# The attention's loads of K, Q, V and the bias table move from SP's DMA queue to GpSimd's

## The chip, the core and the metric

The kernel runs on one core of a Trainium2 chip. PE (TensorE) multiplies matrices and loads its weights beside that (PEld); DVE (VectorE), ACT (ScalarE) and POOL (GpSimd) work on tiles in on-chip memory; SP (SyncE) issues DMAs. Each engine works through its own instructions in order, and waits on semaphores for the others. The metric is the device time of one execution in microseconds (us), less is better.

## What is computed

Two groups of tokens (512 and 2048, treated as five chunks of 512: chunk 0 is the prompt, chunks 1 to 4 are the sample) go through one encoder layer of width 1024. One projection of the normed input gives all branch inputs and gates. Branch A is neighbourhood attention of eight heads on a grid 64 tokens wide (each query sees a window of 8 x 16), branch B the real part of a 2-D DFT, branch C a gated depthwise convolution of width 31. The three are merged under sigmoid gates.

```python
def encoder_layer(x, ...):
    h = rms_norm(x, pre_g)
    z = h @ w_in
    (q, k, v, gate_a, u_b, gate_b, c_val, c_glu, gate_c,
     merge_a, merge_b, merge_c) = jnp.split(z, split_pts, axis=-1)
    y_a = neighbourhood_attention(heads(q), heads(k), heads(v), rpb) * jax.nn.silu(gate_a)
    y_b = fourier_mix(u_b) * jax.nn.silu(gate_b)
    y_c = conformer_conv(c_val, c_glu, dw_w, dw_b, cn_g, cn_b) * jax.nn.silu(gate_c)
    merged = (jax.nn.sigmoid(merge_a) * (y_a @ w_a)
              + jax.nn.sigmoid(merge_b) * (y_b @ w_b)
              + jax.nn.sigmoid(merge_c) * (y_c @ w_c))
    return x + rms_norm(merged @ w_o, post_g)
```

All is float32; the big products are made of three matmuls of split operands (a high part and a remainder).

## The kernel before

**Projections.** `narrow` (L171 to L182) and `wide` multiply the normed chunks `hT` with weights; an output block of `narrow`, 128 x 512, takes 24 matmuls, eight each of L178, L179 and L180. Weights come by `emit_unit` (L138): SP loads 512 KB into a ring `wraw` of three buffers (L142), and ACT and DVE split them (L134, L135). Projections go in three stages: chunks 1 and 2, then 3 and 4, then 0. Each stage makes K, Q, V, the DFT's input and the gates and writes them to DRAM.

**Attention.** `attention(c)` reads them back, for each of eight heads and in each for four column blocks: `load` brings K (`ksp`, L524), Q (`qsp`, two DMAs, L528) and the bias table (`tab`, L530) of the next head, `load_v` brings V (`vsp`) by 8 DMAs of 64 KB (L540) in chunks 2 and 3, by 16 DMAs (L545) in the others. POOL adds table and mask to a `bias` (L560 in chunks 2 and 3, L563 in the others; two buffers, one block ahead). PE multiplies Q and K (L592, tile `s`), DVE adds the bias and takes the maximum `m` (L596), ACT exponentiates and scales (L600, L602), PE transposes (L623), DVE splits (L626), PE multiplies with V (L634), and SP stores the result (L644).

**DFT.** `fft` loads its input (`fu`, L664), and then works in units: a table `w` of 1 MB (L730, one buffer), a matmul L750 (`hp`, in the same two PSUM buffers as the attention's `s`), a second L765, additions on DVE, and a store of the result `yb` (L789). It runs for two halves of the channels, once for chunks 1 to 4 (five units a half), and then for chunk 0 (two units a half).

**Norms.** `rstd_rows` writes the norms of a chunk to DRAM (`rs`, L211), `make_h` reads them back as a row in all partitions (`rrow`, L217), and DVE multiplies the input with it (L221).

**What sets the order.** Projections call `pump()` every few matmuls, and `pump` lets side tasks (attention, convolution, DFT, norms) emit their next piece in proportion. A task has a first and a last step: the attention of chunk 1 is spread over 240 steps, that of chunks 2, 3 and 4 together over 280, that of chunk 0 over 56, and the DFT of chunk 0 comes at the end. What is emitted in this order is then scheduled: the framework simulates the program and sets from that the order of each engine's instructions, so a change of an instruction's engine can move others. Tiles wait for the readers of their buffer's last content.

**The merge.** After chunk 0's projections come the merge and the last projection (`prepare` with L801 to L807, `merge`, `finish`), whose matmuls of `ysp` and `wb` (L178 to L180 in the shape 128x256) begin the stage. Their weights `wb` (L1051) share the ring `wraw` with the projections' weights.

Of the kernel before, what the change touches and what calls it, by code (L numbers as in the profile page):

```python
# [15 lines left out]
F32 = mybir.dt.float32  # L16
# [87 lines left out]
class Build:  # L104
# [399 lines left out]
    def attention(self, c):  # L504

        nc, pool = self.nc, self.ap
        nq, trow, krow = PATS[c]
        n, rows = nq * P, 4 * nq
        kds, vds = self.kds[c > 0], self.vds[c > 0].rearrange("(r w) d -> r w d", w=64)
        grouped = nq == 4  # L510
        mask = pool.tile([P, 3, 512], BF16, tag="mask", name="mask", bufs=1)
        nc.sync.dma_start(mask, self.a["mask"][MASKPAT[c]])
        tq, vq, ahead = [], [], []
        tabs, qk, vs, obs = {}, {}, {}, {}

        def load(hh):


            if hh > 7:
                return  # L520
            j, h = hh // 2, hh % 2
            ksp = pool.tile([P, 16 * 64], F32R, tag="ksp", name="ksp", bufs=2)
            src = kds[j, h].rearrange("i p t -> (i p) t")[:, krow * 64: krow * 64 + rows * 64]
            nc.sync.dma_start(ksp[:, :rows * 64].bitcast(F32), src)  # L524
            qsp = pool.tile([P, 2, C], F32R, tag="qsp", name="qsp", bufs=2)
            src = self.qd[c][j][:, h * 64: h * 64 + 64].rearrange("i p t -> p i t")
            for half in (slice(0, 64), slice(64, P)):
                nc.sync.dma_start(qsp[half].bitcast(F32), src)  # L528
            tb = pool.tile([P, 6, 16, 8], F32, tag="tab", name="tab", bufs=2)
            nc.sync.dma_start(tb, self.a["tab"][hh])  # L530
            qk[hh] = ksp, qsp.rearrange("p i (b q) -> p i b q", b=4)
            tabs[hh] = tb

        def load_v(hh):

            cols = slice(hh * P, hh * P + P)
            vsp = pool.tile([P, 12, P], F32R, tag="vsp", name="vsp", bufs=2)
            if grouped:
                for g in range(8):
                    nc.sync.dma_start(vsp[:, g].bitcast(F32), vds[krow: krow + rows, 8 * g: 8 * g + 8, cols])  # L540
            else:
                for cb in range(4):
                    for r in range(4):
                        src = vds.rearrange("(q r) w d -> r w q d", r=4)
                        nc.sync.dma_start(  # L545
                            vsp[32 * r: 32 * r + 32, nq * cb: nq * cb + nq].bitcast(F32),
                            src[r, KSTART[cb]: KSTART[cb] + 32, krow // 4: krow // 4 + nq, cols])
            vs[hh] = vsp

        def biases():  # L550
            for hh in range(8):
                for cb in range(4):
                    bias = pool.tile([P, 512], F32, tag="bias", name="bias", bufs=2)
                    g0 = RCOL[cb] // 8
                    t = tabs[hh][:, g0: g0 + 4, trow: trow + rows]
                    m, b = mask[:, COLPAT[cb], :n], bias[:, :n]
                    if grouped:
                        m, b = (x.rearrange("p (g r w) -> p g r w", g=4, w=8) for x in (m, b))
                        m, b, t = (x.rearrange("p g r w -> p g (r w)") for x in (m, b, t))
                        nc.gpsimd.tensor_tensor(b, t, m, op=ALU.add)  # L560
                    else:
                        m, b = (x.rearrange("p (r g w) -> p g r w", g=4, w=8) for x in (m, b))
                        nc.gpsimd.tensor_tensor(b, t, m, op=ALU.add)  # L563
                    yield bias

        gen = biases()

        def make_bias():
            return next(gen, None)

        load(0)
        ahead.append(make_bias())
        for _ in range(3):
            yield
        for hh in range(8):
            ksp, qsp = qk.pop(hh)
            for cb in range(4):
                if cb == 1:
                    load(hh + 1)
                if cb == 2:  # L580
                    load_v(hh)
                if cb % 2 == 0:
                    pv = self.ps.tile([P, 2, 2, P], F32, tag="o", name="pv", bufs=1)
                if cb == 0:
                    obs[hh] = pool.tile([P, C], F32, tag="o", name="ob", bufs=2)
                bias = ahead.pop(0)
                ahead.append(make_bias())
                s = self.ps.tile([P, 512], F32, tag="s", name="s", bufs=2)
                kk = ksp.rearrange("p (r c) -> p r c", c=64)[:, :rows, KSTART[cb]: KSTART[cb] + 32]
                if grouped:  # L590
                    kk = kk.rearrange("p r (g w) -> p g r w", w=8)
                nc.tensor.matmul(s[:, :n], lhsT=qsp[:, 0, cb], rhs=kk, start=True, stop=False)  # L592
                nc.tensor.matmul(s[:, :n], lhsT=qsp[:, 1, cb], rhs=kk, start=False, stop=True)
                p = pool.tile([P, 512], F32, tag="p", name="p", bufs=3)
                m = pool.tile([P, 4], F32, tag="m", name="m", bufs=4)
                nc.vector.tensor_tensor_reduce(  # L596
                    out=p[:, :n], in0=s[:, :n], in1=bias[:, :n], scale=1.0, scalar=-3e38,
                    op0=ALU.add, op1=ALU.max, accum_out=m[:, 0:1])
                nc.vector.tensor_scalar_mul(m[:, 1:2], m[:, 0:1], -1.0)  # L599
                nc.scalar.activation(p[:, :n], p[:, :n], AF.Exp, bias=m[:, 1:2], accum_out=m[:, 2:3])  # L600
                nc.vector.reciprocal(m[:, 3:4], m[:, 2:3])
                nc.scalar.mul(p[:, :n], p[:, :n], m[:, 3:4])  # L602
                tq.append(partial(self.transpose_p, nq, p, c, hh, cb, vs, pv, obs))
                yield
                if len(tq) > 3:
                    vq.append(tq.pop(0)())
                yield
                if len(vq) > 2:
                    vq.pop(0)()
                yield  # L610
        while tq or vq:
            if vq:
                vq.pop(0)()
                yield
            if tq:
                vq.append(tq.pop(0)())
                yield
# [526 lines left out]
```

## Time and profile before

| | |
|---|---|
| median of 3 runs (lowest to highest) | 2137.19 us (2135.92 to 2137.59) |
| the profiled execution's own time | 2136.65 us |
| its span in the trace | 2134.8 us |
| mean granted clock of PE | 0.987 |
| busy: PE, PEld | 2069.1 us (97%), 1775.8 us (83%) |
| busy: DVE, ACT, POOL | 1300.3 us (61%), 795.8 us (37%), 292.8 us (14%) |
| moved by DMA | 389.33 MB, mean 182 GB/s |

The span reaches from the first to the last instruction in the trace; the rest of the execution's own time lies around it. SP is not among the busy engines: an issue of a DMA isn't counted as busy, but it holds the queue for the time that its row gives. The granted clock is a share of full speed: 1 is 2.4 GHz, 0.5 is 1.2 GHz, and what lies between is a mixture within the stretch.

### The profile page before, as it was taken

The numbers are of one execution on the slowest core, as the hardware profiler recorded it, in microseconds if no ns is written. First come the engines' busy times: TensorE is split into PE (matmuls) and PEld (weight loads), VectorE is DVE, ScalarE is ACT, GpSimd is POOL, SyncE is SP. The second block draws the span as 40 slices with busy tenths as digits, with TensorE's granted clock in tenths as the row PEclk, the third lists the DMA queues.
The fourth block names the chain that finished last, engine by engine and source line by source line (L and its number), as shares of the span: only waits on it lengthen the run. The fifth ranks groups of instructions, "written<-read, shape, count | busy, mean of one in ns | idle before, by whom it ended". The sixth has DMA issues, their size and how long they took to land. (4 is left out here: it accounts for less than half of the span.)

```text
span 2134.8 us, 31256 instructions
## 1 busy us (share of the span) xinstructions
PE 2069.1 (97%) x11184; PEld 1775.8 (83%) x11184; DVE 1300.3 (61%) x2850; ACT 795.8 (37%) x1625; POOL 292.8 (14%) x286
## 2 busy tenths in 40 slices
PE   8999999999979999999999969999889999999998
PEld 6889888887867899888888858897778889999997
DVE  6554676556444547686665635887745666666655
ACT  6222243344332215564554635335544311111111
POOL 0000011101000002232221211002100121222211
PEclk9999999999989999999999989999999999999999
DMA  8644444555443536575666676777778765555532
GB/s 299 199 154 162 163 146 147 152 173 159 136 143 115 152 131 177 171 195 173 176 182 185 193 195 193 236 236 219 260 247 300 222 211 173 173 185 171 188 129 77
DMA packets 242091, 389.33 MB, mean 182 GB/s; under 512 B 26784, under 2 KB 140064, under 8 KB 240032
## 3 DMA queue, kind: packets, MB, share of 16 engines
q1 hardware_dynamic: 241936, 387.33, 58.2%
q8 instruction: 89, 1.46, 0.3%
q14 instruction: 66, 0.54, 0.1%
HBM read 284.99 MB, written 109.58 MB: 185 GB/s over the span
## 5 line engine op out<-in xcount | busy, mean ns | idle before, releaser
L178 PE MATMUL mm<-hT,w 128*128 128x512 f32 x1760 | 703.7, 400 | 20.2 <-ACT hT L134 10.9
L180 PE MATMUL mm<-hT,w 128*128 128x512 f32 x1760 | 696.1, 396 | 0.1
L179 PE MATMUL mm<-hT,w 128*128 128x512 f32 x1760 | 695.9, 396 | 0.0
L178 PEld LDWEIGHTS mm<-hT,w 128*128 128x128 f32 x1760 | 333.7, 190 | 88.6 <-ACT hT L134 11.3
L180 PEld LDWEIGHTS mm<-hT,w 128*128 128x128 f32 x1760 | 333.0, 189 | 73.8 <-DVE w L135 1.2
L179 PEld LDWEIGHTS mm<-hT,w 128*128 128x128 f32 x1760 | 333.6, 190 | 66.1 <-DVE hT L242 0.9
L135 DVE TENSOR_TENSOR w<-wraw,w 128x512 fp32r<-128x512 f32 x308 | 222.0, 725 | 176.1 <-ACT w L134 172.3
L134 ACT CAST w<-wraw 128x512 fp32r<-128x512 f32 x308 | 188.5, 618 | 247.3 <-PE mm L180 186.5
L453 DVE SCALAR_TENSOR_TENSOR acc<-cb,cw,acc 128x512 f32<-128x512 f32 (+1 forms) x300 | 237.9, 795 | 2.9
L563 POOL TENSOR_TENSOR bias<-tab,mask 128x384 f32<-128x384 f32 (+1 forms) x96 | 94.3, 984 | 829.7 <-DVE m L596 744.7
L178 PE MATMUL mm<-ysp,wb 128*128 128x256 f32 x640 | 181.1, 283 | 2.7 <-DVE nw_y L116 2.7
L179 PE MATMUL mm<-ysp,wb 128*128 128x256 f32 x640 | 181.0, 283 | 0.0
L180 PE MATMUL mm<-ysp,wb 128*128 128x256 f32 x640 | 180.9, 283 | 0.0
L600 ACT ACTIVATE p<-p,m 128x384 f32<-128x384 f32 (+2 forms) x160 | 102.3, 639 | 184.5 <-DVE m L599 158.6
L596 DVE CUSTOM_DVE_ANT_0 p<-s,bias 128x384 f32<-128x384 f32 (+2 forms) x160 | 92.7, 580 | 86.2 <-PE pt L623 69.2
L560 POOL TENSOR_TENSOR bias<-tab,mask 128x512 f32<-128x512 f32 x64 | 86.1, 1346 | 368.7 <-DVE m L596 356.0
L194 PE MATMUL mm<-w,hT 128*128 128x256 f32 x480 | 134.8, 281 | 0.0
L193 PE MATMUL mm<-w,hT 128*128 128x256 f32 x480 | 134.8, 281 | 0.0
L192 PE MATMUL mm<-w,hT 128*128 128x256 f32 x480 | 134.3, 282 | 0.0
L178 PEld LDWEIGHTS mm<-ysp,wb 128*128 128x128 f32 x640 | 122.4, 191 | 4.3 <-DVE th L831 2.9
L857 PE MATMUL po<-wo,msp 128*128 128x512 f32 x320 | 124.5, 389 | 0.0
L856 PE MATMUL po<-wo,msp 128*128 128x512 f32 x320 | 124.2, 390 | 0.0
(152 smaller groups left out, 2961.7 us busy)
## 6 DMA issues: line engine op xcount, KB each, us to landing
wraw<-wn SPq DMA_DIRECT2D x135, 512.0 KB, 4.5
th<-z SPq DMA_DIRECT2D x120, 256.0 KB, 2.6
th<-th SPq DMA_DIRECT2D x80, 384.0 KB, 3.8
qsp<-qd SPq DMA_DIRECT2D x80, 256.0 KB, 6.2
tab<-tab SPq DMA_DIRECT2D x40, 384.0 KB, 3.9
w<-dftd SPq DMA_DIRECT2D x14, 1024.0 KB, 7.7
vsp<-vds SPq DMA_DIRECT2D x256, 48.0 KB, 2.0
xt<-x SPq DMA_DIRECT2D x20, 512.0 KB, 5.2
```

Source lines behind the costliest of these rows:

```text
L134: nc.scalar.copy(dst[:, 0], src)
L135: return nc.vector.tensor_tensor(dst[:, 1], src, dst[:, 0].bitcast(F32), op=ALU.subtract)
L178: nc.tensor.matmul(ps, lhsT=u[:, 0, s], rhs=r[:, 0], start=n == 0, stop=False)
L179: nc.tensor.matmul(ps, lhsT=u[:, 0, s], rhs=r[:, 1], start=False, stop=False)
L180: nc.tensor.matmul(ps, lhsT=u[:, 1, s], rhs=r[:, 0], start=False, stop=n == len(kts) - 1)
L192: nc.tensor.matmul(ps, lhsT=r[:, 0, q], rhs=w[:, 0, s], start=kt == 0, stop=False)
L193: nc.tensor.matmul(ps, lhsT=r[:, 0, q], rhs=w[:, 1, s], start=False, stop=False)
L194: nc.tensor.matmul(ps, lhsT=r[:, 1, q], rhs=w[:, 0, s], start=False, stop=kt == KT - 1)
L453: nc.vector.scalar_tensor_tensor(acc[:, :n], cb[:, b, e:e + n], wv[:, e:e + 1], acc[:, :n], op0=ALU.mult, op1=ALU.add)
L600: nc.scalar.activation(p[:, :n], p[:, :n], AF.Exp, bias=m[:, 1:2], accum_out=m[:, 2:3])
L856: nc.tensor.matmul(po, lhsT=r[:, 0, q], rhs=w[:, 0], start=kt == 0, stop=False)
L857: nc.tensor.matmul(po, lhsT=r[:, 0, q], rhs=w[:, 1], start=False, stop=False)
```

## The change

The four kinds of loads in `attention` are issued by `nc.gpsimd` and not by `nc.sync`: 24 x 16 V loads in chunks 1, 4 and 0, 16 x 8 in chunks 2 and 3, and for each of 40 heads one of K, two of Q and one of the table, 672 DMAs. Tiles, buffers, the amounts loaded and the emission stay; SP keeps 882 DMAs.

```diff
@@ -521,13 +521,13 @@
-            nc.sync.dma_start(ksp[:, :rows * 64].bitcast(F32), src)
+            nc.gpsimd.dma_start(ksp[:, :rows * 64].bitcast(F32), src)
             qsp = pool.tile([P, 2, C], F32R, tag="qsp", name="qsp", bufs=2)
             src = self.qd[c][j][:, h * 64: h * 64 + 64].rearrange("i p t -> p i t")
             for half in (slice(0, 64), slice(64, P)):
-                nc.sync.dma_start(qsp[half].bitcast(F32), src)
+                nc.gpsimd.dma_start(qsp[half].bitcast(F32), src)
             tb = pool.tile([P, 6, 16, 8], F32, tag="tab", name="tab", bufs=2)
-            nc.sync.dma_start(tb, self.a["tab"][hh])
+            nc.gpsimd.dma_start(tb, self.a["tab"][hh])
@@ -537,12 +537,12 @@
             if grouped:
                 for g in range(8):
-                    nc.sync.dma_start(vsp[:, g].bitcast(F32), vds[krow: krow + rows, 8 * g: 8 * g + 8, cols])
+                    nc.gpsimd.dma_start(vsp[:, g].bitcast(F32), vds[krow: krow + rows, 8 * g: 8 * g + 8, cols])
             else:
                 for cb in range(4):
                     for r in range(4):
                         src = vds.rearrange("(q r) w d -> r w q d", r=4)
-                        nc.sync.dma_start(
+                        nc.gpsimd.dma_start(
                             vsp[32 * r: 32 * r + 32, nq * cb: nq * cb + nq].bitcast(F32),
                             src[r, KSTART[cb]: KSTART[cb] + 32, krow // 4: krow // 4 + nq, cols])
```

Since the framework sets the order of every engine anew, instructions move beside the DMAs themselves. Three places show it.

The first is POOL's queue from chunk 4 into chunk 0, before. The rows are the bias adds (L563: twelve rows of keys in chunk 4, eight in chunk 0) and the channel sums of the convolution (L469):

```order
L563 TENSOR_TENSOR bias<-tab,mask 128x4x12x8 x6
L469 TENSOR_TENSOR both<-acc 128x512
L563 TENSOR_TENSOR bias<-tab,mask 128x4x12x8
L469 TENSOR_TENSOR both<-sq 128x512
L563 TENSOR_TENSOR bias<-tab,mask 128x4x12x8 x25
L563 TENSOR_TENSOR bias<-tab,mask 128x4x8x8 x13
```

POOL's queue holds nothing but tensor operations there. The same queue after, from chunk 4's first block on:

```order
L563 TENSOR_TENSOR bias<-tab,mask 128x4x12x8 x2
L545 DMA vsp<-vds 32x3x128 x26
L563 TENSOR_TENSOR bias<-tab,mask 128x4x12x8
L545 DMA vsp<-vds 32x3x128 x4
L563 TENSOR_TENSOR bias<-tab,mask 128x4x12x8
L545 DMA vsp<-vds 32x3x128 x2
L524 DMA ksp<-kds 128x768
L528 DMA qsp<-qd_67 64x2x512 x2
L563 TENSOR_TENSOR bias<-tab,mask 128x4x12x8
L469 TENSOR_TENSOR both<-acc 128x512
```

The bias adds now share the queue with the loads: 26 V loads stand between the second and the third add.

The second is PE at the end of chunk 0's attention, before. `mm<-hT,w` is a projection, `hp` and `op` belong to the DFT, `pt` and `pv` to the attention:

```order
L623 MATMUL pt<-ident,p 128x128
L634 MATMUL pv<-psp,vsp 128x256 x2
L623 MATMUL pt<-ident,p 128x128
L634 MATMUL pv<-psp,vsp 128x256 x2
L623 MATMUL pt<-ident,p 128x128 x2
L180 MATMUL mm<-hT,w 128x512
L178 MATMUL mm<-hT,w 128x512
L179 MATMUL mm<-hT,w 128x512
L180 MATMUL mm<-hT,w 128x512
L750 MATMUL hp<-w,fgs 128x256 x6
L178 MATMUL mm<-hT,w 128x512
```

Projections stand around each piece of the DFT. The same place after:

```order
L765 MATMUL op<-fhs,cd 128x256 x6
L750 MATMUL hp<-w,fgs 128x256 x6
L634 MATMUL pv<-psp,vsp 128x256 x4
L765 MATMUL op<-fhs,cd 128x128 x6
L750 MATMUL hp<-w,fgs 128x256 x6
L765 MATMUL op<-fhs,cd 128x256 x6
L750 MATMUL hp<-w,fgs 128x256 x6
L765 MATMUL op<-fhs,cd 128x128 x6
L178 MATMUL mm<-hT,w 128x512
```

The DFT's last pieces now follow one another with no projection between. Counted over PE's whole order (projection matmuls of 128x512): between the first and the last score matmul of chunk 4 there are 468 before and 705 after; from the first of chunk 4 to the first of chunk 0 there are 834 in both; between the first and the last score matmul of chunk 0 there are 402 and 648; from the last score matmul to the last of the DFT 163 and 0, and from there to the merge 203 and 120.

The third is SP near the end of chunk 0, before. `wraw<-wn` are projection weights, `yd<-yb` is the store of the DFT's result, the others are loads for the merge and a store of gates (L438):

```order
L801 DMA yl<-ya_83 128x2x256
L142 DMA wraw<-wn 128x1024
L801 DMA yl<-ya_83 128x2x256
L789 DMA yd_77<-yb 128x512
L807 DMA gl<-sg_88 128x2x256
L438 DMA th_92<-z 128x512
```

The weights stand ahead of the store. The same place after:

```order
L789 DMA yd_77<-yb 128x512
L801 DMA yl<-ya_83 128x2x256
L807 DMA gl<-sg_88 128x2x256
L805 DMA yl<-yd_78 128x2x256 x2
L142 DMA wraw<-wn 128x1024
L807 DMA gl<-sg_88 128x2x256
L1051 DMA wraw<-wb 128x1024
```

The last projection weights now stand behind that store.

## Rows read from the trace of the kernel before

**Rows 1.** The page: busy time and share of each engine; GB/s in 40 slices

```profile
PE 2069.1 (97%) x11184; PEld 1775.8 (83%) x11184; DVE 1300.3 (61%) x2850; ACT 795.8 (37%) x1625; POOL 292.8 (14%) x286
...
GB/s 299 199 154 162 163 146 147 152 173 159 136 143 115 152 131 177 171 195 173 176 182 185 193 195 193 236 236 219 260 247 300 222 211 173 173 185 171 188 129 77
```

**Rows 2.** PE's waits: tile and line, awaited line: us in total, times, longest

```profile
PE pt L623 <- DVE m L599: 16.4, 2, 16.1
```

**Rows 3.** Windows: length, busy us of each engine, granted clock, DMA share, GB/s

```profile
1250.00:1300.00 50.00, 33.91 (x164) 28.36 (x163) 17.18 (x51) 17.53 (x43) 7.03 (x8) 0.83 0.62 159
1500.00:1550.00 50.00, 42.00 (x216) 34.85 (x215) 36.94 (x107) 26.44 (x70) 8.61 (x10) 0.93 0.78 257
```

**Rows 4.** Timeline of SP in chunk 4: start, length, line, DMA

```profile
1255.60 12.21 SPq L545 DMA_DIRECT2D vsp<-vds  x11
...
1268.33 0.43 SPq L217 DMA_DIRECT2D rrow<-rs  x1
```

**Rows 5.** Timeline of DVE there; in brackets the wait ahead and its end

```profile
1274.20 1.41 DVE L221 SCALAR_TENSOR_TENSOR xr<-xr,preg,rrow 128x512 f32<-128x512 f32 x2 [19.58 <-DMA rrow<-rs]
```

**Rows 6.** Timeline of SP in chunk 0

```profile
1533.80 4.34 SPq L545 DMA_DIRECT2D vsp<-vdp  x6
...
1538.66 0.43 SPq L664 DMA_DIRECT2D fu<-ud  x1
```

**Rows 7.** Timeline of DVE there

```profile
1543.03 0.76 DVE L656 TENSOR_TENSOR fab<-fu 128x256 f32<-128x256 f32 x2 [9.93 <-DMA fu<-ud]
```

**Rows 8.** Window of line L560 alone, bias adds of chunk 2

```profile
900.00:950.00 50.00, 12.29 (x10) 1.00 0.66 178
```

**Rows 9.** Line L592 in chunks 4, 0: ns min/median/max, first and last start

```profile
L592 PE MATMUL s<-ksp,qsp x32: 337/340/522, 1148.0 to 1305.2; 128*128 128x384 f32 x32
...
L592 PE MATMUL s<-ksp,qsp x32: 279/282/415, 1426.4 to 1573.5; 128*128 128x256 f32 x32
```

**Rows 10.** Timeline of PE where the projections end and the merge begins

```profile
1674.30 0.39 PE L178 MATMUL mm<-hT,w 128*128 128x512 f32 x1
...
1674.98 0.28 PE L178 MATMUL mm<-ysp,wb 128*128 128x256 f32 x1
```

**Rows 11.** Windows of the stages, columns as in rows 3

```profile
1148.00:1305.00 157.00, 140.58 (x697) 118.01 (x696) 80.69 (x228) 80.75 (x187) 32.20 (x32) 0.95 0.66 184
1148.00:1426.00 278.00, 261.04 (x1368) 223.18 (x1367) 176.00 (x421) 127.97 (x277) 34.48 (x34) 0.97 0.69 208
1426.00:1573.00 147.00, 137.47 (x747) 116.25 (x746) 109.15 (x316) 80.28 (x210) 28.26 (x32) 0.98 0.73 231
1426.00:1675.00 249.00, 233.37 (x1186) 195.37 (x1185) 155.07 (x394) 122.05 (x288) 32.63 (x35) 0.97 0.76 247
```

**Rows 12.** DMA issues: tile and source, count, KB each, median us to landing

```profile
wraw<-wn SPq DMA_DIRECT2D x135, 512.0 KB, 4.5
...
rs<-nw_y SPq DMA_DIRECT2D x3, 2.0 KB, 9.1
```

**Rows 13.** Lines L540, L545, SP's issues of V, columns as in rows 9

```profile
L540 SPq DMA_DIRECT2D vsp<-vds x128: 520/596/1769, 803.0 to 1122.9; - x128
...
L545 SPq DMA_DIRECT2D vsp<-vds x256: 302/428/1635, 193.3 to 1303.3; - x128
```

**Rows 14.** POOL's groups by form: busy us, mean ns, idle before and its end

```profile
L560 POOL TENSOR_TENSOR bias<-tab,mask 128x512 f32<-128x512 f32 x64 | 86.1, 1346 | 368.7 <-DVE m L596 356.0 <-DVE m L601 11.3 <-DVE m L599 1.2
...
L563 POOL TENSOR_TENSOR bias<-tab,mask 128x384 f32<-128x384 f32 x64 | 66.8, 1045 | 593.8 <-DVE m L596 528.4 <-DMA tab<-tab 24.4 <-DMA vsp<-vds 14.5
L563 POOL TENSOR_TENSOR bias<-tab,mask 128x256 f32<-128x256 f32 x32 | 27.5, 863 | 235.9 <-DVE m L596 216.3 <-DVE m L601 11.3 <-DMA vsp<-vdp 7.4
```

**Rows 15.** Timeline of PE, the six first matmuls of a DFT unit

```profile
1620.94 0.88 PE L750 MATMUL hp<-w,fgs 128*128 128x256 f32 x6
```

**Rows 16.** Line L730, the loads of `w` from 1500 us on

```profile
DMA to landing us min/median/max: 4.8/8.1/8.9
```

## The prediction, made before the changed kernel had run

> **What bounds the kernel now.** I read the busy times first. PE holds 97% of the span, POOL 14% [rows 1]: what does not lengthen PE's own work or its idle time costs nothing. Next PE's waits: the longest by far is one of 16.1 us before the transposes of L623 [rows 2]. Then the stretches in which PE is not full. Of 50 us it worked 33.9 and 42.0 in two places, and in the same two the granted clock was 0.83 and 0.93, a mixture of the two levels 2.4 and 1.2 GHz [rows 3]. So an idle time is paid twice, once as idle and once as slower work beside it.
>
> Both places hang on the loads that the change moves. In chunk 4, SP spends 12.21 us on issuing eleven V loads, and L217, which loads the row of norms for chunk 0, leaves SP only behind them, at 1268.33 [rows 4]; DVE, whose queue is in order, waits 19.58 us for it [rows 5], and PE waits 16.1 us for DVE. In chunk 0 the load of `fu` stands behind V loads too, the last six of which take 4.34 us of SP [rows 6], and DVE waits 9.93 us for that [rows 7]. POOL's side is light: ten bias adds in 50 us [rows 8], so 20 us for a head (four adds) of chunks 2 and 3.
>
> **What goes.** The score matmuls (L592) of chunk 4 begin at 1148.0 and end at 1305.2, those of chunk 0 run from 1426.4 to 1573.5 [rows 9], and the merge begins at 1674.98 [rows 10]. From chunk 4's first to chunk 0's first there are 278 us, of which PE idles 17.0, and the clock of 0.97 costs 8.3 more (3% of 278); 252.7 us are PE's own work. From there to the merge it is 249 us: 15.6 idle, 7.5 by the clock, 225.9 own [rows 11]. Both kernels have the same matmuls in each of these two stretches (768 projection matmuls of 128x512 in the second, for instance); only their order differs. So the most that could come back is 25.3 + 23.1 = 48.4 us. PE waits for loads of the attention nowhere else, so SP's relief is worth nothing elsewhere.
>
> Not all of the hole in chunk 4 is SP's issuing. L211's write of the norms takes 9.1 us to land [rows 12], and L217's read from 1268.33 to 1274.20; that round trip stays. Of DVE's 19.58 us some 7 are then left (19.58 - 12.21), of PE's 16.1 some 4; I leave 5 us of PE idle time there.
>
> **What comes: POOL.** 672 DMAs move: four a head for K, Q and the table, and for V eight a head in chunks 2 and 3, 16 in the others. No row shows what a DMA costs POOL. The lower bound is what the same V loads cost SP, medians of 0.43 and 0.60 us [rows 13]; the upper is POOL's longest kind of bias add, 1.35 us [rows 14]. I take 1.1 us, for the nearest rows are POOL's own: all its 286 operations have a mean of 292.8/286 = 1.02 [rows 1], its 160 bias adds (86.1 + 66.8 + 27.5)/160 = 1.13 [rows 14]. Now each stage against what PE has to do in it, with t for the price.
>
> Chunks 2 and 3: 12t + 4 x 1.346 is 18.6 us for a head, in 20: it fits. Chunk 1, whose eight heads are spread by the code over 240 steps where chunks 2 to 4 have 24 heads in 280, has room to spare.
>
> Chunk 4: between its first and last score matmul PE had 157 us, without idle time (16.4) and clock (7.9) 132.7 [rows 11]. The new order puts 237 more projection matmuls there (705 for 468), at 0.227 us (three in 1674.30 to 1674.98, [rows 10]) 54 us: 187. POOL has 152 DMAs (128 for V, four each for six heads), 30 adds of 1.045 and two of about 1.4: 152t + 34.2 = 201.4. POOL is later by 14.2 us, and the 5 us from above disappear in that. Chunk 0: PE has 134.6 in the 147 us of before and 246 more matmuls (648 for 402), together 191; POOL 152t + 30 x 0.863 + 2.8 = 195.9; later by 4.7. So POOL becomes the bound where t is over 1.01 in chunk 4 and over 1.07 in chunk 0. PE's queue is in order, so that a POOL which is late there holds PE up, and one which is early gains nothing beyond the idle time.
>
> **What comes: the end of chunk 0.** Here a cover is used up. Before, 163 projection matmuls stand between the last score matmul and the last DFT matmul, and 203 behind it. Now there are none between and 120 behind. DFT units are chained: `w` has one buffer, so each load waits for the unit before. A unit takes 0.9 us of PE [rows 15], 0.4 of issue (as a V load, [rows 13]) and 8.1 of landing [rows 16], 9.4 us; three of these are 28.2. Outside them stand eight operations of ACT and DVE one behind the other (two for L750's result, four for L765's, two for the split of weights), by the 0.7 us of a 128x512 operation [rows 5] 5.6 us. SP, whose order has the store of the DFT's result ahead of the next projection weights, needs three issues, 1.3 us, and the weights 4.5 to land [rows 12]. That is 39.6 us before PE has its next projection. The 120 matmuls take 27.3 us. For the clock beside so much idle time I add 5 us (the hole of chunk 4, half as long, lost 8.3). In all 72 us from the last score matmul to the merge.
>
> **The sum.** First stretch: 252.7 + 14.2 - 278.0 = -11.1. Second: 191.2 + 4.7 + 72.1 - 249 = +19.0. At the start POOL issues the tables of two heads (768 KB) at once, ahead of the first weights; at the 299 GB/s of the first slice [rows 1] they can delay these by 0 to 2.6 us: +1.3. The sum is +9.2 us. Against the profiled execution's own 2136.65 us (span 2134.8; the median of the runs, 2137.19, is 0.5 us more) that is 2146 us.
>
> **Rivals.** (1) POOL issues nearly as cheaply as SP. Speaking for it: SP's rows at 0.43 to 0.60. It decides at t = 1.01, at which 152t + 34.2 equals chunk 4's 187. Below it only the 5 us of DVE's round trip stay: -25.3 + 5 + 14.3 + 1.3 = -4.7, 2132 us. With loads of `w` that land in 4.8 us, the shortest in [rows 16], and no clock loss at the end, the tail is 57 us and the time 2117. The Trainium skill (DMA: Bandwidth & Descriptors, Latency and other measured facts) gives a first byte after about 1 us for a DMA issued by GpSimd, and lays that to its emission of descriptors; if POOL is held for just that time, an estimate from that page, this rival holds. No row here shows it.
>
> (2) POOL is held longer, 1.35 us, as in its longest adds, because it and DVE get in each other's way; this ends slower. For it: DVE is busy 61% of the time [rows 1]. Against it: chunk 4's adds of 384 columns take no more than 1.045 us in all the traffic. It decides from t = 1.22, where 12t + 5.4 fills the 20 us of a head. Then chunk 4 is late by 52.2 us, chunk 0 by 42.7, and the 16 heads of chunks 2 and 3, which need 21.6 us each, by 25: -25.3 + 52.2 + 14.3 + 42.7 + 25 + 1.3 = +110, 2247 us. The Trainium skill (SBUF — State Buffer, SBUF: two separate sides) says that GpSimd can't write the descriptors of a DMA while DVE runs an operation that holds the port pair they share, and gives a DMA of about 620 ns that grew to about 3100; it is this mechanism, and no row here shows how often it would bite.
>
> (3) The tail stays covered, because projections run ahead of the last DFT units after all, so that the order I read is not what decides. Then only POOL's lateness stands against the 48.4 us: -48.4 + 14.2 + 4.7 + 1.3 = -28, 2108 us.
>
> **How the numbers follow.** Forecast (t from 1.06 to 1.21, the tail open; 2135 to 2180): 0.50. Rival 1: 0.27, of it two thirds under 2133. Rival 2: 0.15. Rival 3: 0.08. What a measurement of this kernel can tell from no change is about 0.2%, 4.3 us. Slower by more: 0.42 of the forecast's 0.50 and all of rival 2, 0.57. Within: 0.08 of the forecast and 0.09 of rival 1, 0.17. Faster: 0.18 of rival 1 and all of rival 3, 0.26. The range goes from 2117 (rival 1 with the short tail) to 2215, where t is 1.28; beyond lie rival 3 and most of rival 2.
>
> **What would show it.** In the changed kernel's trace: POOL's DMA issues and their spacing, 1.1 us; the wait of L221 in chunk 4 down from 19.58 to under 10 us, and no long wait for `fu`; POOL's bias adds no longer waiting for DVE's `m` in chunks 4 and 0, and DVE's L596 waiting for `bias` instead; PE with some 30 us of idle time at the DFT's L750 and L765 and at the first projection behind them. The prediction is wrong if a POOL issue is far from 1.1 us, if projections run among the last DFT units, or if PE's new idle time stands in chunks 1 to 3.

## The result, and the profile after

The changed kernel takes 2166.05 us in the median of four runs, the kernel before, run beside it, 2136.56 us: ratio 1.0137, 95% interval 1.0109 to 1.0166. So it is slower by some 29 us; 2146 was forecast, in a range of 2117 to 2215. The profiled execution took 2168.64 us, its span is 2166.9 us, 32.1 us more than before. The four lie between 2159.62 and 2168.89, so a stage, which is read from one execution, is known to a few us.

The page of the changed kernel first (busy time of each engine, the granted clock in tenths, the software queue that is new). It answers [rows 1]:

```profile
PE 2076.5 (96%) x11184; PEld 1780.0 (82%) x11184; DVE 1313.2 (61%) x2850; ACT 799.3 (37%) x1625; POOL 653.2 (30%) x958
...
PEclk9999999999999999999999999999996999999999
...
q0 software_dynamic: 30208, 78.69, 13.6%
```

POOL is busy for 360 us more and still stands at 30%. The clock has one dip, at slice 31 of 40, 1625 to 1679 us: the end of chunk 0. PE's waits say the same (tile and line, awaited line, us in total, times, longest; [rows 2] has the first of before):

```profile
PE mm L178 <- ACT w L134: 23.1, 2, 15.8
PE pv L634 <- issue: 14.4, 1, 14.4
PE mm L178 <- ACT hT L134: 10.0, 1, 10.0
PE hp L750 <- DMA w<-dftd: 8.4, 3, 3.4
PE pt L623 <- ACT p L602: 6.9, 4, 3.1
PE pv L634 <- DVE ob L640: 5.0, 1, 5.0
```

The 16.1 us before L623 are gone, and so are 7.9 us before it in chunk 0, behind the late `fu` of [rows 7]:

```profile
PE pt L623 <- DVE psp L626: 7.9, 1, 7.9
```

New are 15.8 us at a projection, 14.4 us at a PV matmul, and several of 3 to 5 us. The stages are bounded as in the prediction, by the first and last score matmul ([rows 9]) and the first matmul of the merge ([rows 10]):

```profile
L592 PE MATMUL s<-ksp,qsp x32: 337/340/689, 1157.3 to 1368.2; 128*128 128x384 f32 x32
...
L592 PE MATMUL s<-ksp,qsp x32: 280/282/390, 1440.2 to 1630.9; 128*128 128x256 f32 x32
```

```profile
L178 PE MATMUL mm<-ysp,wb x640: 278/283/415, 1702.9 to 2137.5; 128*128 128x256 f32 x160
```

| stage | before | after | difference | forecast |
|---|---|---|---|---|
| start to chunk 4's first score matmul | 1148.0 | 1157.3 | +9.3 | +1.3 |
| from there to chunk 0's first | 278.4 | 282.9 | +4.5 | -11.1 |
| chunk 0's first to last | 147.1 | 190.6 | | |
| from there to the merge | 101.5 | 72.0 | | |
| the last two together | 248.6 | 262.6 | +14.0 | +19.0 |
| merge to the end | 459.8 | 464.0 | +4.2 | 0 |
| sum | 2134.8 | 2166.9 | +32.1 | +9.2 |

Windows of the changed kernel answer [rows 11] (length, PE, PEld, DVE, ACT and POOL busy, granted clock, DMA share, GB/s):

```profile
1157.00:1440.00 283.00, 265.80 (x1371) 223.87 (x1370) 180.78 (x422) 128.51 (x278) 115.56 (x178) 0.99 0.67 205
1440.00:1631.00 191.00, 190.83 (x1002) 162.11 (x1001) 127.47 (x335) 99.10 (x237) 105.62 (x184) 1.00 0.75 232
...
1631.00:1703.00 72.00, 45.53 (x186) 36.50 (x185) 33.23 (x59) 27.38 (x52) 4.48 (x3) 0.72 0.70 236
```

Between chunk 0's first and last score matmul PE is full at full clock, and POOL busy for 105.6 us of 191. POOL is nowhere the bound. Behind the last score matmul PE idles for 26.5 us of 72 at a clock of 0.72.

How much of a low clock falls on work, its own window shows. Before, all time at half speed between chunk 4's first score matmul and chunk 0's is one piece:

```profile
1264.80:1281.90 17.10, 3.42 (x10) 2.97 (x11) 5.63 (x16) 4.60 (x13) 1.78 (x2) 0.50 0.75 189
```

PE works for 3.42 us of it; the rest lies in the hole of 16.1 us.

**The price on POOL.** The line of the V loads, and one burst in POOL's timeline:

```profile
L545 POOL DMA_DIRECT2D vsp<-vds x256: 545/545/680, 191.3 to 1361.3; - x128
```

```profile
1206.20 7.03 POOL L545 DMA_DIRECT2D vsp<-vds  x13 [2.30 <-PE pv L634]
1213.49 1.75 POOL L545 DMA_DIRECT2D vsp<-vds  x3 [0.26 <-DMA vsp<-vds]
```

A DMA holds POOL for 0.545 us (7.03/13 = 0.54 in a row), against 0.43 of SP for the same load [rows 13] and against the 1.1 us that the prediction took.

**The end of chunk 0.** PE's timeline from the last score matmul on, and SP's beside it:

```profile
1631.10 0.88 PE L750 MATMUL hp<-w,fgs 128*128 128x256 f32 x6
...
1637.46 1.31 PE L750 MATMUL hp<-w,fgs 128*128 128x256 f32 x6
...
1643.77 1.62 PE L750 MATMUL hp<-w,fgs 128*128 128x256 f32 x6 [3.42 <-DMA w<-dftd]
...
1650.34 1.65 PE L750 MATMUL hp<-w,fgs 128*128 128x256 f32 x6 [1.98 <-DMA w<-dftd]
...
1671.48 0.79 PE L178 MATMUL mm<-hT,w 128*128 128x512 f32 x1 [15.81 <-ACT w L134]
```

```profile
1656.69 0.33 SPq L789 DMA_DIRECT2D yd<-yb  x1
...
1666.38 0.46 SPq L142 DMA_DIRECT2D wraw<-wn  x1
```

The four last DFT units stand bare, 6.3 to 6.6 us apart. Then SP stores the result (L789), and the weights leave 9.7 us behind the store. Between them stand loads for the merge (L801, L805, L807). They don't read what was just stored: the merge begins with chunk 1, so L805 reads `yd_78`, and the store writes chunk 0's `yd_77`. SP's waits from 1656.1 to 1666.5 us:

```profile
SPq L801 <- DMA yl<-ya: 2.8, 1, 2.8
SPq L805 <- POOL yl L802: 1.9, 1, 1.9
SPq L801 <- POOL yl L802: 1.4, 1, 1.4
SPq L805 <- DVE ysp L135: 0.9, 1, 0.9
```

These are 7.0 of the 9.7 us: the loads wait until the merge's tiles `yl` (three buffers) are filled, added by POOL, split by DVE and free again, and the projection weights stand behind them in the queue.

**The row of norms.** DVE's timeline at L221, in chunk 1's attention and in chunk 4's ([rows 5] is the latter before):

```profile
487.76 2.08 DVE L221 SCALAR_TENSOR_TENSOR xr<-xr,preg,rrow 128x512 f32<-128x512 f32 x3 [16.31 <-DMA rrow<-rs]
...
1257.84 1.42 DVE L221 SCALAR_TENSOR_TENSOR xr<-xr,preg,rrow 128x512 f32<-128x512 f32 x2 [9.55 <-DMA rrow<-rs]
```

In chunk 4 the wait fell from 19.58 to 9.55 us, but SP's issuing of V was the smaller part of it. One of SP's waits of before from 1253 to 1269 us, and the landing of the write of the norms (L211), which left SP at 1254.40 there:

```profile
SPq L545 <- DMA rs<-nw_y: 5.4, 1, 5.4
```

```profile
DMA to landing us min/median/max: 11.1/11.1/11.1
```

So the 12.21 us of [rows 4] are not all issuing: eleven issues of some 0.43 us are 4.7, and 5.4 us are the wait of one V load until that write had landed, at 1265.5 (the two signal the same semaphore). L217 could not have left earlier either; it left 2.8 us later. In the changed kernel the write takes 11.1 us again and L217 leaves with its landing. Of the 10.0 us by which the wait fell, 2.8 are SP's queue, 1.0 is a faster landing of the read, and 6.2 are DVE's order: before, DVE came to L221 0.2 us behind the write's issue, now it comes 6.4 us behind it.

In chunk 1 the wait was 10.11 us before and cost PE next to nothing; now it is 16.31 and costs PE 14.43. It is longer because the write lands after 13.0 us (9.1 before) and the read after 7.2 (5.5); no run shows why. That it now costs PE, the order shows. DVE's queue there, before and after:

```
L626 TENSOR_TENSOR psp<-pt,psp 128x3x128
L453 SCALAR_TENSOR_TENSOR acc<-cb,cw,acc 128x497
L640 TENSOR_TENSOR ob<-pv,ob 128x2x8x16
L297 TENSOR_TENSOR z<-mm,rows 128x512
L453 SCALAR_TENSOR_TENSOR acc<-cb,cw,acc 128x497
L135 TENSOR_TENSOR w<-wraw,w 128x512
L221 SCALAR_TENSOR_TENSOR xr<-xr,preg,rrow 128x512 x3
```

```
L221 SCALAR_TENSOR_TENSOR xr<-xr,preg,rrow 128x512 x3
L626 TENSOR_TENSOR psp<-pt,psp 128x3x128
L453 SCALAR_TENSOR_TENSOR acc<-cb,cw,acc 128x497
L640 TENSOR_TENSOR ob<-pv,ob 128x2x8x16
```

L626 and L640, on which the next PV matmul waits, stood ahead of the waiting L221 and now stand behind it.

### The profile page after: what moved, and what is told of

Read it like the earlier page. It is cut to its first block, busy times and chain, and to the rows that moved or that the text cites. A ratio compares the mean times of both kernels' runs of the same rounds, so it can differ in the third digit from the quotient of the medians.

```text
span 2166.9 us, 31250 instructions
## 1 busy us (share of the span) xinstructions
PE 2076.5 (96%) x11184; PEld 1780.0 (82%) x11184; DVE 1313.2 (61%) x2850; ACT 799.3 (37%) x1625; POOL 653.2 (30%) x958
## 5 line engine op out<-in xcount | busy, mean ns | idle before, releaser
L563 POOL TENSOR_TENSOR bias<-tab,mask 128x384 f32<-128x384 f32 (+1 forms) x96 | 91.1, 952 | 315.1 <-DVE m L596 288.0
L545 POOL DMA_DIRECT2D vsp<-vds x256 | 139.1, 550 | 153.4 <-DVE w L135 108.6
L834 POOL TENSOR_TENSOR th<-th 128x256 f32<-128x256 f32 x80 | 69.4, 868 | 284.4 <-DVE th L831 143.8
L626 DVE TENSOR_TENSOR psp<-pt,psp 128x384 fp32r<-128x384 f32 (+2 forms) x160 | 92.3, 579 | 55.7 <-ACT psp L625 55.1
```

The costliest lines, as they stand in the source:

```text
L545: nc.gpsimd.dma_start(vsp[32 * r: 32 * r + 32, nq * cb: nq * cb + nq].bitcast(F32), src[r, KSTART[cb]: KSTART[cb] + 32, krow // 4: krow // ...
```

## The experiments

Theory A: the loss is one of order. The scheduler sets the order of each chunk's attention anew, and at a few places work that PE needs comes to stand behind a long wait, or loses the projections that covered it. Theory B: the loss is one of POOL as an issuer of DMAs, so it goes with their number and is spread. Line numbers in these kernels are higher by one, in those with the row of norms on chip by six. Stage lengths, taken as in the table above, from each kernel's profiled execution (c4 and c0 are the first score matmuls of chunks 4 and 0):

| kernel | ratio to before (95%) | to c4 | c4 to c0 | c0 to merge | merge to end |
|---|---|---|---|---|---|
| before | | 1148.0 | 278.4 | 248.6 | 459.8 |
| after | 1.0137 (1.0109 to 1.0166) | 1157.3 | 282.9 | 262.6 | 464.0 |
| only0 | 1.0061 (1.0040 to 1.0083) | 1146.8 | 277.3 | 264.9 | 459.9 |
| only1 | 1.0045 (1.0030 to 1.0060) | 1154.0 | 276.7 | 247.0 | 462.6 |
| only4 | 1.0030 (1.0018 to 1.0042) | 1147.6 | 286.1 | 244.2 | 461.8 |
| only23 | 1.0013 (1.0001 to 1.0025) | 1144.2 | 278.7 | 246.6 | 463.0 |
| v_all | 1.0020 (1.0011 to 1.0029) | 1153.4 | 273.8 | 245.6 | 462.1 |
| after_perow | 1.0064 (1.0046 to 1.0082) | 1133.0 | 288.2 | 262.0 | 463.0 |
| before_perow | 0.9906 (0.9889 to 0.9923) | 1135.4 | 269.4 | 246.9 | 463.7 |
| after_ydq | 1.0118 (1.0103 to 1.0133) | 1155.5 | 283.8 | 252.1 | 469.1 |
| after_hpmm | 1.0127 (1.0107 to 1.0147) | 1156.3 | 237.1 | 309.3 | 462.9 |
| before_hpmm | 1.0017 (1.0003 to 1.0032) | 1144.3 | 266.5 | 262.3 | 462.8 |
| after_perow_hpmm | 1.0024 (1.0014 to 1.0033) | 1132.8 | 278.4 | 265.3 | 462.8 |
| before_perow_hpmm | 0.9921 (0.9906 to 0.9935) | 1135.4 | 259.1 | 262.6 | 460.0 |

**One chunk at a time.** In `attention` the queue is chosen by chunk; here for chunk 0:

```diff
+        kq, tbq, vq_ = ((nc.gpsimd if c in (0,) else nc.sync) for _ in range(3))
-            nc.sync.dma_start(ksp[:, :rows * 64].bitcast(F32), src)
+            kq.dma_start(ksp[:, :rows * 64].bitcast(F32), src)
```

and so for Q, the table (`tbq`) and V (`vq_`). 

> Only chunk 0's 160 loads are issued by POOL, the others by SP as before; PE's order has the changed kernel's counts in chunk 0 (648 projection matmuls between its score matmuls, 0 ahead of the last DFT matmul, 120 behind) and the old ones in chunk 4. Theory A, the loss comes from the order that the scheduler sets around chunk 0's late score matmuls: the stretch from chunk 0's first score matmul to the merge is longer by 14 us, the merge by 0 to 4, so +14 to +18 us against before, 2151 to 2155 us. Theory B, each DMA issued by POOL costs the same wherever it stands (29.5 us for 672): 160/672 of it, +7 us, 2144 us.

> Only chunk 1's 160 loads are issued by POOL. PE's counts of matmuls between the marks are those of before. Theory A: the new wait of 14.4 us at a PV matmul near 480 us comes back, because the matmul stands close behind DVE's wait for the row of norms, and with it +9 us, 2146 us; chunk 4 and the end stay as before. Theory B: 160/672 of 29.5, +7 us. The two are told apart by the place: a single wait near 480 us for A, many small waits for B.

> Only chunk 4's 160 loads are issued by POOL; PE's order has 705 projection matmuls between chunk 4's score matmuls, and the old order in chunk 0 and at the end. Theory A: the 16 us hole at L221 is gone, small waits on late DFT input and norms take its place as in the changed kernel, +4 us, 2141 us, and chunk 0 and the end stay as before. Theory B: +7 us, 2144 us, with the hole's return not explained.

> Only the 192 loads of chunks 2 and 3 are issued by POOL; PE's counts are those of before. Theory A: nothing waits there before or after, 0 us (within 4), 2137 us. Theory B: it has the most DMAs, 192/672 of 29.5, +8 us, 2145 us.

Measured against before, with medians of before at 2134.67: only0 +13.0 us, only1 +9.6, only4 +6.4, only23 +2.8 (each ratio less 1, times that median). They add up to 31.8, the whole change to 29.3. The 192 loads of chunks 2 and 3, which are the most, cost the least, and each of the others lengthens its own stage, and no other by more than 3.2 us: in the table the stage from c0 to the merge grows in only0 alone (+16.3), that from c4 to c0 in only4 alone (+7.7), that from the start in only1 alone (+6.0). Theory B falls as a price for each DMA. only1 also brings back the single wait, 10.0 us at the same PV matmul (PE's waits in only1):

```profile
PE pv L635 <- issue: 10.0, 1, 10.0
```

only0 lies just under what Theory A gave (14 to 18), only4 and only23 some 2 to 3 us above it.

**V alone.** K, Q and tables stay with SP (`kq` and `tbq` are `nc.sync`, `vq_` is `nc.gpsimd` in all chunks). 

> The V loads of all chunks are issued by POOL (512 DMAs), K, Q and tables by SP. PE's order stands between the two kernels: 614 projection matmuls between chunk 4's score matmuls (468 before, 705 changed), 642 matmuls between chunk 0's (492, 738, both forms of projection counted), 96 between the last score matmul and the last DFT matmul (163, 0), 120 behind. Theory A: the end is covered by these 96 (22 us of PE), so the stretch from chunk 0's first score matmul to the merge is 248 to 254 us (before 248.6, changed 262.6); the waits of chunks 1 and 4 stay, in all +8 to +16 us against before, 2145 to 2153 us. Theory B: 512/672 of 29.5, +22 us, 2159 us.

It came out at +0.2%, 4 us, better than both expected. 512 of the 672 DMAs are on POOL, 128 of them in chunk 0, and yet the stretch from c0 to the merge is 245.6 us, 3 us shorter than before. The 96 projection matmuls between the last score matmul and the last DFT matmul cover the DFT's units, but not the whole end: the wait for the last projection weights stays, with the same loads of the merge ahead of them in SP's queue. PE's timeline, and the window of the stretch, in v_all:

```profile
1641.35 0.79 PE L178 MATMUL mm<-hT,w 128*128 128x512 f32 x1 [14.66 <-ACT w L134]
```

```profile
1427.00:1673.00 246.00, 228.98 (x1185) 194.71 (x1184) 161.37 (x389) 125.58 (x287) 98.36 (x163) 0.96 0.76 247
```

PE idles for 17.0 us here, for 15.6 before [rows 11] and for 26.6 in the changed kernel. So the wait for the weights takes about the place of the holes that went (7.9 us of them behind the late `fu`), and the 10 us more of the changed kernel are its waits in the bare chain of the DFT (10.1 us between 1631 and 1656). The stretch from the start keeps +5.4 us.

**The row of norms made on chip.**

```diff
-        nc.sync.dma_start(self.rs[c].rearrange("o (t p) -> p (o t)", p=P), r)
+        self.rv[c] = r
...
-        nc.sync.dma_start(rrow, self.rs[c].to_broadcast([P, C]))
+        ps = self.ps.tile([P, C], F32, tag="s", name="rrow", bufs=2)
+        for t in range(4):
+            dg = self.zp.tile([P, C], F32, tag="z", name="dg")
+            nc.vector.tensor_scalar_mul(dg[:, :P], self.ident, self.rv[c][:, t:t + 1])
+            nc.tensor.matmul(ps[:, t * P: t * P + P], lhsT=self.one, rhs=dg[:, :P], start=True, stop=True)
+        nc.scalar.copy(rrow, ps)
```

> The changed kernel, but the row of norms of chunks 3, 4 and 0 is made on chip (four matmuls with a diagonal, as the kernel already does for chunks 1 and 2) and not written to DRAM and read back. Theory A (the waits of 14.4 us near 480 us and of 5.0 us in chunk 4 hang on that round trip of 11 + 5 us, and on what stands behind it in DVE's queue): both waits go, and with them the 10 us at the first projection of chunk 3, 20 to 29 us less than the changed kernel, 2137 to 2146 us; the end of chunk 0 keeps its 72 us. Theory B (the waits come from slow loads of POOL): at most the 10 us, the others stay, 2156 us or more.

> The kernel before with the same edit: all loads on SP, the row of norms made on chip. Theory A: the hole of 16.1 us in chunk 4 and the 10.9 us at the first projection of chunk 3 go, and about 8 us of lower clock beside them; with some of it taken by the next late thing, 20 to 33 us less than before, 2104 to 2117 us. If the hole of chunk 4 was SP's issuing of V and not the round trip, DVE still waits for something behind the V loads there: only some 11 us less, 2126 us.

In the changed kernel it takes off 15.6 us (1.0137 to 1.0064, of 2135.4), less than the 20 to 29 expected. The stretch to c4 is shorter by 24.3 us, about the two waits there of 14.4 and 10.0 us (2.1 of the second stay); but the stretch from c4 to c0, where 5.0 were to go, grew by 5.3. PE waits there in small pieces for the softmax (L608, six of the seven waits and 7.2 us of this row of PE's waits in after_perow):

```profile
PE pt L629 <- ACT p L608: 7.9, 7, 4.0
```

PE's idle time in this stretch is the same 17.0 us, but it works 16.9 us at half speed where the changed kernel works 6.6, and that is the growth. The order in chunk 4 changed with the edit (560 projection matmuls between the score matmuls, 705 in the changed kernel), so what the row alone gives there is not separated. In the kernel before the edit takes off 20 us (0.9906), the lower end of what was expected: 12.6 ahead of c4 and 10.7 from c4 to the merge, which is itself 3.9 us longer. With before_perow_hpmm, from which its interval does not part it, it is the fastest kernel run here. PE's waits in before_perow have neither the 16.1 nor the 10.9 us, though SP issues all V loads:

```profile
PE mm L178 <- ACT w L134: 7.3, 3, 5.6
PE pt L629 <- DVE psp L632: 6.2, 2, 6.0
```

So the hole of chunk 4 before was the round trip of the norms.

**Loads of the stored result taken off SP.**

```diff
-                nc.sync.dma_start(y, self.yd[c][2 * b2 - 4: 2 * b2 - 2, :, tok].rearrange("b p t -> p b t"))
+                nc.gpsimd.dma_start(y, self.yd[c][2 * b2 - 4: 2 * b2 - 2, :, tok].rearrange("b p t -> p b t"))
```

> The changed kernel, but the merge's loads of the stored DFT results (yl from yd) are issued by POOL, so that SP no longer waits for the last store's landing ahead of the last projection weights. Theory A: PE's wait of 15.8 us at the first projection behind the DFT shrinks by the 9 us which SP spends between that store and the weights, the end of chunk 0 from 72 to some 63 us, 9 us less than the changed kernel, 2157 us. If the weights wait for something else (a free buffer of the ring, the DMA rate), no change, 2166 us.

SP's timeline, PE's, and one of SP's waits from 1655.2 to 1662.6 us in after_ydq:

```profile
1655.28 0.35 SPq L790 DMA_DIRECT2D yd<-yb  x1
...
1662.50 0.35 SPq L142 DMA_DIRECT2D wraw<-wn  x1
```

```profile
1666.66 0.80 PE L178 MATMUL mm<-hT,w 128*128 128x512 f32 x1 [12.78 <-ACT w L134]
```

```profile
SPq L142 <- DVE wb L135: 2.4, 1, 2.4
```

The expectation took SP's 9.7 us for a wait until the store had landed; as shown above, the two loads wait for tiles of the merge (1.9 and 0.9 us). With them gone the weights leave 7.2 us behind the store and not 9.7, now after a wait of their own for DVE (the row of SP's waits above), and PE is back 36.6 us behind the last score matmul (1630.06), not 40.6. The stretch to the merge fell by 10.7 us, from 72.0 to 61.3; but the new order leaves 98 projection matmuls there and not 120, and the other 22, 5 us, run in the merge, which is 5.1 us longer. So 5.6 of the 9 us came in the profiles; by the ratio (1.0118) it is 4, which the intervals do not part from none.

**The DFT off the score matmuls' PSUM ring.**

```diff
-                hp = self.ps.tile([P, 512], F32, tag="s", name="hp", bufs=2)
+                hp = self.ps.tile([P, 512], F32, tag="mm", name="hp", bufs=3)
```

> The changed kernel, but the DFT's first product (hp) takes its PSUM buffers from the projections' ring (mm, three buffers) and not from the score matmuls' ring (s, two), so that the scheduler no longer puts the DFT behind chunk 0's late score matmuls: the four last DFT units stand among projections, 53 projection matmuls lie between the last score matmul and the last DFT matmul and 211 behind (changed kernel 0 and 120). All loads stay with POOL at the same price. Theory A (the end of chunk 0 is slow because the order leaves the DFT chain uncovered): the 72 us from the last score matmul to the merge, 31 of them without cover, fall to what the matmuls there need, 25 to 31 us less than the changed kernel, 2135 to 2141 us. Theory B (POOL's queue makes chunk 0 late): the order is not what decides, 2155 us or more.

> Control: the same edit of the PSUM ring in the kernel before, where the DFT already stands among projections. Theory A: no gain beyond the single wait of 3.7 us at L750, 0 to -4 us, 2131 to 2136 us. If it gains as much here as in the changed kernel, the ring cost both kernels and says nothing on the change.

> The changed kernel with both edits (row of norms on chip, the DFT's ring). Theory A: both gains add up, 15 us for the row as measured in after_perow and 25 to 31 for the ring, 2120 to 2126 us. If it is still above the kernel before, something else in the change costs time.

> The kernel before with both edits: the row gave 20 us (before_perow), the ring should give 0 to 4, 2111 to 2115 us. Its distance to after_perow_hpmm is what the move to POOL is worth once neither order hurts: Theory A 5 to 15 us against POOL, 0 or below if the relief of SP is worth something.

This one missed. The order moved as wanted and the bare chain of units is gone, but the time is that of the changed kernel (1.0127). From c4 to the merge it takes 546.4 us, where the changed kernel has 545.5 and before 527.0 (before_hpmm 528.8). Two windows, the first ahead of the last score matmul and the second behind it, in after_hpmm:

```profile
1393.00:1633.00 240.00, 217.64 (x1181) 187.35 (x1180) 165.78 (x419) 110.89 (x262) 106.83 (x184) 0.94 0.74 237
1633.00:1703.00 70.00, 68.12 (x307) 56.37 (x307) 36.02 (x63) 32.68 (x62) 5.55 (x4) 0.94 0.73 246
```

Now PE is nearly full behind the last score matmul and idles ahead of it, 22.4 us at a clock of 0.94. PE's longest waits of that stretch in after_hpmm:

```profile
PE mm L178 <- DVE fhs L756: 5.4, 4, 1.6
PE hp L751 <- DMA w<-dftd: 4.0, 3, 2.1
PE pt L624 <- ACT p L603: 3.8, 3, 1.3
```

They are many and short, on the DFT and the softmax, none on POOL or on a tile that POOL loads. What the cover gave back the clock took. The stretches at half speed between c4 and the merge sum up alike in both kernels, but PE works in more of them (the sums of length and PE, after_hpmm and the changed kernel):

```profile
sum 47.80, PE 39.89 PEld 33.05 DVE 27.15 ACT 22.57 POOL 17.92; mean PE 4.99 PEld 4.13 DVE 3.39 ACT 2.82 POOL 2.24
```

```profile
sum 47.90, PE 23.92 PEld 18.99 DVE 24.86 ACT 16.09 POOL 8.76; mean PE 5.98 PEld 4.75 DVE 6.22 ACT 4.02 POOL 2.19
```

PE idles 36.4 us from c4 to the merge and not 43.8, some 7 less, but works 16.0 us more at half speed, which loses some 8. So covering the DFT's units is not enough by itself. The control moved by +3.6 us (1.0017) where 0 to -4 was expected, and so the ring is no gain for either kernel alone; with the row of norms on chip it takes 8.5 us off the changed kernel (1.0064 to 1.0024). With both edits the changed kernel gains 24 us (1.0024), where 40 to 46 were expected. Between after_perow_hpmm and before_perow_hpmm (0.9921) lie 22 us, more than the 5 to 15 of Theory A: with both edits POOL's version still loses, and loses it between c4 and the merge (543.7 us against 521.7).

## Why the prediction came out as it did

- **The hole of chunk 4** (right in its numbers, not in its reason). DVE's wait for the row was to fall under 10 us and PE to keep 5: 9.55 and 5.04. But of the 12.21 us that were to go with SP's V loads only 2.8 had held L217 back; 6.2 us came from DVE's new order, which the prediction does not name, and that was luck. And the claim that this was all that stayed was wrong: from c4 to c0 PE idles 17.2 us (283.0 - 265.8), as much as before, in pieces of 1 to 5 us. Beside the 5.04 the longest are 3.09 at 1238 us, behind a softmax that ACT had held back for a load of `xt`, 2.66 at 1336, behind DVE's wait of 7.56 us for `fu`, and 3.00 at the DFT's first `w`. None of them is in the sum. Without POOL's lateness the forecast for this stretch is 257.7 us (252.7 + 5), and 282.9 were measured: of the 25.2 us between, 12.2 are this idle time beyond the 5, 2.8 the clock (1%), 6.6 the next point, and what is left, some 4, no row explains.
- **"So an idle time is paid twice"** (wrong for this hole). The clock of 0.97 was to have cost 8.3 us beside the 17.0 of idle time. But of the 17.1 us at half speed (the window of before above) 13.7 are the idle time itself, and PE works for 3.42: these lose 1.7 us, and PE's own work is 259.3 us and not 252.7. Counted so, the second stretch loses 5.3 us by the clock and not 7.5 (PE works 4.02 and 6.54 us of it at half speed), and the most that could come back is 39.6 us and not 48.4.
- **POOL's price** (the mis-sized term). 1.1 us was taken and 0.545 measured. With that POOL needs 152 x 0.545 + 34.2 = 117 us in chunk 4 and 112 in chunk 0, against 187 and 191 of PE: the 14.2 and the 4.7 us of lateness don't exist. The nearest row was SP's 0.43 to 0.60 for the same DMA [rows 13], named as the lower bound; POOL's adds, whose duration goes with what they compute, were no measure of a queue's issue. By this term rival 1 held (t under 1.01), and its 2132 us were missed by 34.
- **The Trainium skill's two rules.** The trace shows POOL held for 0.52 to 0.75 us over all 672 DMAs while DVE is busy 61%: the 278 that fell wholly into DVE's busy time have a median of 0.545 us, the 150 that fell wholly into its idle time 0.547. The growth from about 620 to about 3100 ns that the Trainium skill describes (SBUF — State Buffer, SBUF: two separate sides) shows nowhere in this time. It is given there for a copy of DVE, and only one of the 672 met a copy here (0.533 us), so the trace does not try it much. The first byte after about 1 us that the Trainium skill gives (DMA: Bandwidth & Descriptors, Latency and other measured facts) is not the time for which POOL is held. POOL's loads do land later than SP's (3.6 us in the median for 48 KB, 2.0 by SP), and no run shows why.
- **The tail** (right in sum, by two errors that cancel). 72.1 us were forecast and 72.0 measured, and PE's return after 39.6 and 40.6 us. But three units take 19.2 us (1631.10 to 1650.34), not 28.2, since most of a load's landing lies beside the unit ahead; and SP takes 9.7 us from the store to the weights, not 1.3. The order was read rightly (store, loads, weights), but the loads were priced as issues, and they wait for the merge's tiles `yl`.
- **Chunk 0's attention** (195.9 forecast, 190.6 measured). PE's own work of 191 us was right; the 4.7 us of POOL were not there. That the late `fu` would go was right too: DVE waits 4.7 us for it at most here, not 9.93.
- **The start** (+1.3 forecast, +9.3 measured). The two early tables cost nothing: the first score matmul comes at 170.1 us, 170.5 before. What failed is the sentence that SP's relief is worth nothing elsewhere because PE waits for loads nowhere else. It holds for the loads; but I compared the order on PE, POOL and SP only from chunk 4 on, and not DVE's in chunk 1, where a wait of 10 us already stood, hidden by two operations that had been put ahead of it.
- **The merge** (0 forecast, +4.2 measured). It takes 459.8 to 463.7 us in kernels that keep all loads of chunk 0 on SP, too, so the change is not shown to be its cause.
- **The sum.** With POOL's true price the steps of the prediction give rival 1's -4.7 us. What it left out is 25.2 us between c4 and c0, 8.0 at the start and 4.2 in the merge, 37 in all, and that is the measured +32. The 14.2 and 4.7 us that POOL did not cost stood in for part of it, so that sign and range came out right by a term that was wrong; of the steps that made the forecast slower only the tail's is borne out. Of the three signs that were to show the prediction wrong, two came: an issue far from 1.1 us, and new idle time of PE in chunk 1 (14.43 us).

**What the runs settle, and what they don't.** Shown: the loss is made chunk by chunk (only0, only1, only4, only23), does not go with the number of DMAs, and is not POOL's time. Shown too: in chunk 1 it is L221's wait with the attention's operations behind it, since the wait goes with the round trip (after_perow). For chunk 0 the runs show that the loss goes along with the bare chain of the DFT behind the late score matmuls: v_all, with three quarters of the DMAs on POOL, an order between the two and the wait for the weights, loses nothing there, and no wait of PE, DVE or ACT in chunk 0 of the changed kernel names POOL or a tile that it loads. That the order alone is the cause is argued, not shown: no run has POOL's loads in the order of before, and after_hpmm says that easing one piece of the order is not enough. K, Q and the tables alone on POOL were not run either: PE's waits for the softmax (`p`, L602) come to 6 to 12 us in all kernels that have all of chunk 4's loads on POOL, to 2.5 before, and v_all has none. In chunk 4 not even that much goes together: v_all has 614 projection matmuls between the score matmuls and takes 273.8 us from c4 to c0, after_perow has 560 and takes 288.2, before 468 and 278.4. Which of the order and the later landing of POOL's loads (3.6 us in the median for 48 KB, 2.0 by SP) makes the small waits there stays open.

## What to carry over

Where a framework sets the order from its own prices, moving DMAs to another queue is first a change of order: compare every engine's order, and look for waits that cost nothing today because what PE needs happens to stand ahead of them. Size an issue by the nearest issue, not by the engine's other work. A row of a queue's timeline that merges several issues can hold a wait: divide its length by the price of one issue before you blame the issues. Clock lost while PE idles anyway costs nothing; count what PE did at half speed. And a DMA that reads back what was just stored holds its whole queue for the landing (SP at L217, in the changed kernel):

```profile
SPq L217 <- DMA rs<-nw_y: 28.4, 3, 11.3
```

Taking such a round trip away (the row of norms, 0.9% in the kernel before) was worth more than moving any of the loads to another queue was here.

## What the hardware showed

A DMA held POOL for 0.54 to 0.61 us in the median of each line, whatever it moved: 0.545 for V loads of 48 KB (L545), 0.558 for K (L524), 0.607 for Q (L528), 0.572 for tables of 384 KB (L530). That is near SP's 0.43 to 0.60 and far from POOL's adds of 0.86 to 1.35 us, and DVE's work beside it did not lengthen it (in the median 0.545 us with DVE busy throughout, 0.547 with DVE idle):

```profile
L524 POOL DMA_DIRECT2D ksp<-kds x32: 536/558/643, 76.2 to 1317.3; - x32
...
L528 POOL DMA_DIRECT2D qsp<-qd x80: 594/607/695, 80.3 to 1602.5; - x80
...
L530 POOL DMA_DIRECT2D tab<-tab x40: 559/572/697, 1.3 to 1585.8; - x40
```

The write of the norms, 2 KB, takes longer to land than the large loads do in the median: 8.5 to 13.0 us here, 7.5 to 11.1 before ([rows 12] has the median), where the 1 MB tables of the DFT take 7.3.
